# Rotary scores kernel: one GpSimd load and one GpSimd store around DMA engine 4 in place of five GpSimd loads

## The chip, the cores and the metric

The kernel runs on one core of a Trainium2 chip. The metric is the device time of one execution in microseconds (us): the median of three runs is 793.6 us (792.91 to 794.66). A difference between two kernels is told as a time and as a share of this.

## What is computed

From the reference, cut to what matters. `q` and `k` are [16, 512, 16, 64] in float32 (batch, sequence, heads, dim); `cos` and `sin` are [512, 32].

```
q1, q2 = q[..., :half_dim], q[..., half_dim:]
q_rot = np.concatenate([q1 * cos_q - q2 * sin_q, q1 * sin_q + q2 * cos_q], axis=-1)
...                                   (k_rot from k in the same way)
scores = np.einsum('bshd,bthd->bsht', q_rot, k_rot)
```

The inputs are 67 MB. The output, [16, 512, 16, 512] in float32, is 268 MB, so four fifths of all the bytes that move are stores of scores.

## The kernel before

**Tiling.** A batch of `q` or `k` is loaded by one transfer as 128 partitions of four sequence rows each, 16 KB to a partition, 2 MB in all (`load`, L113 to L122). Partition p holds the sequence rows 4p to 4p + 3; c counts these four. The work goes in 64 steps, i = 4 * batch + c. A step takes the 128 q rows of one c against all 512 k rows, for 16 heads, and fills one stage tile `st` of 128 partitions by 32 KB (4 MB), which one transfer stores to the output (`store`, L187 to L188).

**One step** (the last loop of the kernel): for each of eight pairs of heads `scores` (L190 to L213) has TensorE make two products of 64x128 by 64x512 into a PSUM tile `ps` (L201), and ScalarE copies both to `st` in one instruction of 128x1024 (L208). Between these, TensorE transposes later rows of q and k (L170), VectorE and ScalarE copy those from PSUM (L185), and VectorE makes the rotation in three operations on 128x1024 (L149, L150, L154). At the end of a step with c = 2 the next but one batch of q is loaded, and at the end of a step with c = 3 a batch of k; so step 18 issues the load of q6, step 19 that of k7, step 38 that of q11, step 39 that of k12 and step 54 that of q15 ("q6" is batch 6 of q).

**What sets the order.** The order of each engine's instructions is written out by hand (`manual_schedule`). Ordinary loads and stores are all issued by SyncE's queue in program order; each waits there for what it needs: a store for the last copy into its stage tile, a load for the last reader of its buffer. There are three stage tiles, so the first copy of step i waits until the store of step i - 3 has landed. q and k have two input buffers each. Steps 0 to 3 (batch 0) are stored in 16 pieces of 1 MB (L211) and loaded in smaller units; steps 4 to 63 make the 60 stores of L188.

**Engines and rows.** A transfer is carried by the core's DMA engines in parallel. A load or store of 128 rows gives each of the sixteen engines eight rows. The name `SLOW = 4` in the code (L75) is the number of one engine, and five loads are treated so that this one gets less:

- `RELIEVED` (L74) lists them: q6, k7, q11, k12, q15, numbered 0 to 4.
- `load_around` (L86 to L111) issues rows 0 to 119 of such a load on GpSimd's queue. A GpSimd transfer of 120 rows is carried by fifteen engines, eight rows each, that follow each other from a cursor; the cursor stands behind the last one afterwards. Before the first such load the cursor is reset (L101); `move_cursor(n)` (L78 to L84) shifts it by n engines with a tiny transfer of n rows into `scratch`, which nobody reads. `move_cursor(SLOW + 1)` sets it to 5, so the fifteen engines are 5 to 15 and 0 to 3.
- `halves` (L94 to L98) cuts each row of 16 KB in two pieces of 8 KB, the second first.
- The left rows 120 to 127: for a load with an even number (q6, q11, q15) SyncE issues them as a transfer of eight rows (L111); for an odd one (k7, k12) GpSimd issues them in halves, with the cursor set to 8 by `move_cursor(8)` (L105 to L107).

Of the kernel before, what the change touches and what calls it, by code (L numbers as in the profile page):

```python
# [10 lines left out]
def kernel(  # L11
# [8 lines left out]
    nc = tc.nc  # L20
# [4 lines left out]
    B, S, H, D = q.shape  # L25
    HD = D // 2
    P = 128
    C = S // P
# [14 lines left out]
    dram = {  # L43
        "q": q.rearrange("b (p c) h d -> b p c h d", c=C),
        "k": k.rearrange("b (p c) h d -> b p c h d", c=C),
    }
    o_v = out.rearrange("b (p c) h t -> b c p h t", c=C)
# [23 lines left out]
    batches = {}  # L71

    RELIEVED = {("q", 6): 0, ("k", 7): 1, ("q", 11): 2, ("k", 12): 3, ("q", 15): 4}  # L74
    SLOW = 4  # L75
    scratch = const_pool.tile([P, 96], fp32, name="scratch")
    tiny = [0]

    def move_cursor(n):

        y = tiny[0]
        tiny[0] += 1
        src = bass.AP(q.tensor, 512 * y, [(512, n), (64, 2), (1, 2)])
        nc.gpsimd.dma_start(scratch[:n, 4 * y : 4 * y + 4].rearrange("p (a b) -> p a b", a=2), src)  # L84

    def load_around(which, b, t):  # L86

        n, E, F = 120, C * H * D, C * H * D // 2  # L90
        x = RELIEVED[which, b]
        d = dram[which][b]

        def halves(lo, hi):  # L94
            src = bass.AP(d.tensor, d.offset + lo * E + F, [(E, hi - lo), (-F, 2), (1, F)])
            v = t[lo:hi].rearrange("p c e -> p (c e)")
            dst = bass.AP(v.tensor, v.offset + F, [v.ap[0], (-F, 2), (1, F)])
            nc.gpsimd.dma_start(dst, src)  # L98

        if x == 0:  # L100
            nc.gpsimd.inc_swdge_sem([], [], mode="reset_dge_cursor")  # L101
        else:

            move_cursor(16 - SLOW)
        if x % 2:  # L105
            move_cursor(8)
            halves(n, P)  # L107
        move_cursor(SLOW + 1)
        halves(0, n)
        if not x % 2:  # L110
            nc.sync.dma_start(t[n:].rearrange("p c (h d) -> p c h d", h=H), d[n:])  # L111

    def load(which, b):  # L113

        if b >= B:
            return
        t = in_pool.tile([P, C, H * D], fp32, tag=which + "_in", name=which + "_sb")
        batches[which, b] = t
        if (which, b) in RELIEVED:
            load_around(which, b, t)  # L120
        else:
            nc.sync.dma_start(t.rearrange("p c (h d) -> p c h d", h=H), dram[which][b])  # L122

# [61 lines left out]
        copy(out=dst, in_=src)  # L185

    def store(i, st):  # L187
        nc.sync.dma_start(o_v[i // C, i % C], st)  # L188

    def scores(i, p, st):  # L190

        ps = ps_s_pool.tile([P, 2, S], fp32, tag="ps_s", name="ps")
        b = i // C
        if b == 0:
            c, hp = divmod(p, 2)
            lhs, rhs = qT[i][:, C * hp + c], kT[0][:, 2 * i + hp]
        else:
            lhs, rhs = qT[i][:, p], kT[b][:, p]
        for r in range(2):
            po, rh = ps[:, r, :], rhs[64 * r : 64 * r + 64, :]  # L200
            nc.tensor.matmul(  # L201
                out=po, lhsT=lhs[64 * r : 64 * r + 64, :], rhs=rh, start=True, stop=True
            )
        so, si = st[:, 2 * p : 2 * p + 2, :], ps
        if b > 0:
            so = so.rearrange("s r (t c) -> s r t c", c=C)
            si = si.rearrange("s r (c t) -> s r t c", c=C)
        nc.scalar.copy(out=so, in_=si)  # L208
        if b == 0 and p % 2 == 1:
            c = p // 2  # L210
            nc.sync.dma_start(o_v[0, c, :, G * i : G * (i + 1)], st[:, G * c : G * (c + 1)])  # L211
        elif b > 0 and p == HP - 1:
            store(i, st)  # L213
# [9 lines left out]
    with tc.manual_schedule():  # L223
        for t, src in ((cos_t, cos), (sin_t, sin)):
            nc.scalar.dma_start(t, src.rearrange("(p c) j -> p c j", c=C))
        for head, heads in ((0, G), (G, H - G)):
            load_units("k", head, heads)
            load_units("q", head, heads)
        load("k", 1)
        load("q", 1)  # L230
        make_identity(nc, ident)
        nc.scalar.copy(out=ss_t[:, :, 0, :], in_=sin_t)
# [6 lines left out]
        for i in range(C):  # L239
            st = st_first[i] if i < 2 else stage_pool.tile([P, H, S], fp32, tag="stage", name="st")  # L240
            if i < C - 1:
                dve = rope("k", i + 1) + rope("q", i + 1) + rope("k", C + i)
                nxt = [("k", i + 1), ("q", i + 1)]
            else:
                dve = rope("q", C) + rope("k", C + i) + rope("q", C + 1) + rope("k", 2 * C)
                nxt = [("q", C), ("k", C + i)]
            for p in range(HP):
                scores(i, p, st)
                if p in (0, 1) and i > 0:
                    run(dve[:1])  # L250
                    dve = dve[1:]
                    transposed("k", C + i - 1, p, nc.vector.tensor_copy)
                if p == 3 and i < 2:
                    load("kq"[i], 2)
                if p in (2, 6):
                    m = len(dve) - (4 if p == 2 else 2) - (2 if i == C - 1 else 0)
                    run(dve[:m])
                    dve = dve[m:]
                    tr_act(*nxt.pop(0))
            run(dve)  # L260
# [3 lines left out]
        for i in range(C, NST):  # L264
# [10 lines left out]
            st = stage_pool.tile([P, H, S], fp32, tag="stage", name="st")  # L275
# [45 lines left out]
```

## Time and profile before

| | |
|---|---|
| runs, median (lowest to highest) | 793.6 us (792.91 to 794.66) |
| profiled execution, first to last instruction | 790.4 us, 3.2 us below the median of the runs |
| TensorE matmul busy | 684.4 us (87% of the span) |
| VectorE busy | 544.7 us (69%) |
| ScalarE busy | 562.0 us (71%) |
| GpSimd busy | 11.9 us (2%) |
| bytes moved by DMA | 336.18 MB, mean 425 GB/s |
| read from and written to HBM | 67.24 MB and 268.44 MB |
| stores of 4 MB: number, median time from issue to landing | 60, 24.7 us |
| loads on SyncE of 2 MB | 13 of k, 28.3 us; 12 of q, 26.5 us |
| loads on GpSimd of 1920 KB (120 rows) | 3 of q, 27.8 us; 2 of k, 43.3 us |

How to read it. The profile is that of one execution; its span runs from the first to the last instruction of the program, and the runs' time includes what lies around it. The busy share of an engine is a mean over all stages. The profile's page has the engines' busy shares in 40 slices of the span, and the mean busy share of the sixteen DMA engines in the same slices; a part on the DMA queues, where q1 is SyncE's queue and q0 GpSimd's; the chain of work that ended last; groups of equal instructions; and transfers with the time from issue to landing. The trace answers further questions: who waited for whom and how long, what was issued when, the busy times within a stretch of the span, and the records of the single DMA packets (start, duration, size and queue). A row of a transfer is one packet, or two when it is cut in halves.

### The profile page before, as it was taken

What the parts mean: (1) busy time and instruction counts of PE and PEld (TensorE: products, weight loads), DVE (VectorE), ACT (ScalarE), POOL (GpSimd) and SP (SyncE); (2) the same over time, 40 slices, a digit from 0 to 9 for tenths busy, and PEclk for the clock granted to TensorE, in tenths of its full rate; (3) what the DMA queues carried; (4) which work ended last, traced back from release to release, by engine and by line L of the source; (5) the groups of instructions that cost most, each with busy time, mean ns of one, the idle gap of its engine ahead of it and who ended that gap; (6) DMA issues with size and microseconds to landing.
All of it is one profiled execution on the core that took longest, in us unless ns stands there. A gap on an engine that the chain in (4) does not pass through costs nothing.

```text
span 790.4 us, 7750 instructions
## 1 busy us (share of the span) xinstructions
PE 684.4 (87%) x3072; PEld 296.4 (38%) x3072; DVE 544.7 (69%) x516; ACT 562.0 (71%) x647; POOL 11.9 (2%) x24
## 2 busy tenths in 40 slices
PE   4989998988988889798996989889899798799960
PEld 2444443433433334343342433334334343344420
DVE  6999988666766678576785767667678487587400
ACT  3888886865857768486785866777577586588770
POOL 0000000000001000000000001000000000000000
PEclk9999999998999999898998989999899899899995
DMA  9999999999999999999999999999999999999997
GB/s 357 417 425 439 429 430 435 425 435 436 429 429 428 413 432 419 433 423 438 433 427 436 426 432 429 422 432 424 430 432 427 436 429 432 430 432 434 432 429 340
DMA packets 18836, 336.18 MB, mean 425 GB/s; under 512 B 2312, under 2 KB 3592, under 8 KB 4616
## 3 DMA queue, kind: packets, MB, share of 16 engines
q1 hardware_dynamic: 16704, 325.46, 96.4%
q0 software_dynamic: 1808, 10.10, 3.1%
q8 instruction: 24, 0.39, 0.2%
q10 hardware_dynamic: 288, 0.13, 0.1%
q14 instruction: 12, 0.10, 0.0%
HBM read 67.24 MB, written 268.44 MB: 425 GB/s over the span
## 4 chain that ended last, share of the span: by engine, by line
DMA 49%; PE 40%; ACT 5%; DVE 3%; issue 1%; ACTq 0%; SPq 0%; DVEq 0%
DMA out_dram<-st 46%; PE ps L201 30%; PE bank L170 10%; ACT st L208 5%; DMA q_sb<-in_q_dram 2%; DVE part L149 1%; DMA early<-in_k_dram 1%; DVE q_sb L150 0%; DVE k_sb L154 0%; DVE k_sb L150 0%; DVE q_sb L154 0%; DVE early L150 0%; DVE kT_t L185 0%; ACTq L316 0%; DVE early L154 0%
## 5 line engine op out<-in xcount | busy, mean ns | idle before, releaser
L208 ACT COPY st<-ps 128x1024 f32<-128x1024 f32 x512 | 495.7, 1020 | 192.6 <-DMA out_dram<-st 109.8
L201 PE MATMUL ps<-kT_t,qT_t 64*128 64x512 f32 x2048 | 544.0, 649 | 67.0 <-ACT st L208 67.0
L201 PEld LDWEIGHTS ps<-kT_t,qT_t 64*128 64x128 f32 x2048 | 183.6, 196 | 256.2 <-issue 133.3
L185 DVE COPY qT_t<-bank 128x512 f32<-128x512 f32 x118 | 81.6, 691 | 193.9 <-PE bank L170 193.9
L170 PEld LDWEIGHTS bank<-ident,q_sb 128*128 128x128 f32 x480 | 54.2, 149 | 99.0 <-issue 96.4
L170 PEld LDWEIGHTS bank<-ident,k_sb 128*128 128x128 f32 x480 | 50.3, 140 | 96.4 <-DVE k_sb L150 39.5
L170 PE MATMUL bank<-ident,q_sb 128*128 128x128 f32 x480 | 85.1, 304 | 0.9 <-PE ps L201 0.9
L170 PE MATMUL bank<-ident,k_sb 128*128 128x128 f32 x480 | 78.5, 286 | 1.6 <-DVE qT_t L185 1.2
L185 ACT COPY kT_t<-bank 128x512 f32<-128x512 f32 x122 | 72.4, 598 | 6.4 <-PE bank L170 6.4
L154 DVE TENSOR_TENSOR k_sb<-k_sb,part 128x1024 f32<-128x1024 f32 x60 | 73.5, 1225 | 2.1
L150 DVE TENSOR_TENSOR q_sb<-q_sb,cos_t 128x1024 f32<-128x1024 f32 x60 | 73.5, 1225 | 2.1
L150 DVE TENSOR_TENSOR k_sb<-k_sb,cos_t 128x1024 f32<-128x1024 f32 x60 | 73.5, 1225 | 2.0
L149 DVE TENSOR_TENSOR part<-q_sb,ss_t 128x1024 f32<-128x1024 f32 x60 | 73.5, 1225 | 2.0
L149 DVE TENSOR_TENSOR part<-k_sb,ss_t 128x1024 f32<-128x1024 f32 x60 | 73.0, 1216 | 0.9 <-DMA k_sb<-in_k_dram 0.7
L154 DVE TENSOR_TENSOR q_sb<-q_sb,part 128x1024 f32<-128x1024 f32 x60 | 72.9, 1216 | 0.0
L170 PE MATMUL bank<-ident,early 128*128 128x128 f32 x64 | 10.5, 315 | 12.4 <-DVE early L154 10.5
L170 PEld LDWEIGHTS bank<-ident,early 128*128 128x128 f32 x64 | 8.3, 161 | 17.4 <-issue 13.4
L149 DVE TENSOR_TENSOR part<-early,ss_t 128x1024 f32<-128x1024 f32 x8 | 9.8, 1222 | 5.8 <-DMA early<-in_k_dram 5.7
L98 POOL DMA_DIRECT2D q_sb<-in_q_dram x3 | 2.3, 752 | 620.2 <-PE bank L170 446.2
L154 DVE TENSOR_TENSOR early<-early,part 128x512 f32<-128x512 f32 x16 | 10.3, 687 | 0.2
L150 DVE TENSOR_TENSOR early<-early,cos_t 128x1024 f32<-128x1024 f32 x8 | 9.8, 1225 | 0.3
L185 ACT COPY qT_t<-bank 128x512 f32<-128x512 f32 x10 | 5.7, 629 | 3.2 <-PE bank L170 3.2
(12 smaller groups left out, 15.9 us busy)
## 6 DMA issues: line engine op xcount, KB each, us to landing
out_dram<-st SPq DMA_DIRECT2D x60, 4096.0 KB, 24.7
k_sb<-in_k_dram SPq DMA_DIRECT2D x13, 2048.0 KB, 28.3
q_sb<-in_q_dram SPq DMA_DIRECT2D x12, 2048.0 KB, 26.5
out_dram<-st SPq DMA_DIRECT2D x16, 1024.0 KB, 13.8
q_sb<-in_q_dram POOLq DMA_DIRECT2D x3, 1920.0 KB, 27.8
k_sb<-in_k_dram POOLq DMA_DIRECT2D x2, 1920.0 KB, 43.3
early<-in_k_dram SPq DMA_DIRECT2D x1, 1536.0 KB
early<-in_q_dram SPq DMA_DIRECT2D x1, 1536.0 KB
```

Source lines behind the costliest of these rows:

```text
L98: nc.gpsimd.dma_start(dst, src)
L149: nc.vector.tensor_tensor(pv, xs, ss, op=mult)
L150: nc.vector.tensor_tensor(xc, xc, cs, op=mult)
L154: nc.vector.tensor_tensor(y, y, z, op=add)
L170: nc.tensor.transpose(bank[:, x, :], src, ident)
L185: copy(out=dst, in_=src)
L201: nc.tensor.matmul(out=po, lhsT=lhs[64 * r : 64 * r + 64, :], rhs=rh, start=True, stop=True)
L208: nc.scalar.copy(out=so, in_=si)
```

## The change

Only one load, q11, still goes around engine 4, as before: rows 0 to 119 in halves on GpSimd, the rows 120 to 127 by SyncE. q6, k7, k12 and q15 become ordinary loads of 128 rows on SyncE's queue. In their place the store of step 30 goes around it: rows 0 to 119 are issued on GpSimd in halves, 16 KB each here, with the cursor at 5, and the left rows by SyncE in two transfers of four rows, 120 to 123 and 124 to 127. The store comes first in program order, so the reset of the cursor stands before it, and q11 shifts the cursor by 12 and by 5. Of eighteen transfers on GpSimd's queue five are left: the two of 120 rows and three tiny ones. The function `load_around` becomes `around`, which takes a destination and a source.

```diff
-    RELIEVED = {("q", 6): 0, ("k", 7): 1, ("q", 11): 2, ("k", 12): 3, ("q", 15): 4}
     SLOW = 4
+    AROUND = 120
+    RELIEVED_LOADS = {("q", 11)}
+    RELIEVED_STORES = {30}
...
+    def around(dst, src):
+        def halves(t):
+            f = t.ap[1][1] // 2
+            return bass.AP(t.tensor, t.offset + f, [t.ap[0], (-f, 2), (1, f)])
+
+        if relieved[0] == 0:
             nc.gpsimd.inc_swdge_sem([], [], mode="reset_dge_cursor")
         else:
             move_cursor(16 - SLOW)
-        if x % 2:
-            move_cursor(8)
-            halves(n, P)
+        relieved[0] += 1
         move_cursor(SLOW + 1)
-        halves(0, n)
-        if not x % 2:
-            nc.sync.dma_start(t[n:].rearrange("p c (h d) -> p c h d", h=H), d[n:])
+        nc.gpsimd.dma_start(halves(dst[:AROUND]), halves(src[:AROUND]))
...
-        if (which, b) in RELIEVED:
-            load_around(which, b, t)
+        if (which, b) in RELIEVED_LOADS:
+            d = dram[which][b].rearrange("p c h d -> p (c h d)")
+            around(t.rearrange("p c e -> p (c e)"), d)
+            nc.sync.dma_start(t[AROUND:].rearrange("p c (h d) -> p c h d", h=H), dram[which][b][AROUND:])
...
     def store(i, st):
-        nc.sync.dma_start(o_v[i // C, i % C], st)
+        o = o_v[i // C, i % C]
+        if i in RELIEVED_STORES:
+            around(o.rearrange("p h t -> p (h t)"), st.rearrange("p h t -> p (h t)"))
+            for lo in (AROUND, AROUND + 4):
+                nc.sync.dma_start(o[lo : lo + 4], st[lo : lo + 4])
+        else:
+            nc.sync.dma_start(o, st)
```

More of the change, by code (lines that the diff above doesn't have):

```diff
@@ L71 @@
     batches = {}
-    RELIEVED = {("q", 6): 0, ("k", 7): 1, ("q", 11): 2, ("k", 12): 3, ("q", 15): 4}
     SLOW = 4
+    AROUND = 120
+    RELIEVED_LOADS = {("q", 11)}
+    RELIEVED_STORES = {30}
     scratch = const_pool.tile([P, 96], fp32, name="scratch")
     tiny = [0]
+    relieved = [0]
     def move_cursor(n):
@@ L84, in move_cursor @@
         nc.gpsimd.dma_start(scratch[:n, 4 * y : 4 * y + 4].rearrange("p (a b) -> p a b", a=2), src)
[L86 to L100, printed above, removed]
+    def around(dst, src):
[3 more added lines that the diff above has]
+        if relieved[0] == 0:
             nc.gpsimd.inc_swdge_sem([], [], mode="reset_dge_cursor")
```

## The prediction

> **What bounds the kernel now.** I read the page's second and third parts, then the waits, the stage windows, SyncE's timeline, and last the trace's packet records.
>
> ```profile
> span 790.4 us, 7750 instructions
> ...
> DMA  9999999999999999999999999999999999999997
> ...
> q1 hardware_dynamic: 16704, 325.46, 96.4%
> q0 software_dynamic: 1808, 10.10, 3.1%
> ```
>
> The first row is the span, DMA the busy share of the sixteen DMA engines in 40 slices. The queue rows (packets, MB, share of sixteen engines' span) add up with the three small ones to 99.8%: 788.8 of 790.4 us for the mean engine. No engine has time to spare, so the end is total work over sixteen, plus what the latest engine has more than the mean.
>
> ```profile
> ACT st L208 <- DMA out_dram<-st: 109.8, 42, 5.7
> SPq L188 <- ACT st L208: 659.7, 60, 16.7
> ...
> 225.00:310.00 85.00, 76.88 (x343) 32.74 (x340) 59.93 (x56) 62.45 (x73) 4.89 (x8) 0.94 1.00 424
> 310.00:381.00 71.00, 62.47 (x272) 26.71 (x272) 49.46 (x46) 49.32 (x57) 0.00 (x0) 0.90 1.01 432
> 767.00:790.00 23.00, 0.00 (x0) 0.00 (x0) 0.00 (x0) 0.83 (x1) 0.00 (x0) 0.53 0.84 360
> ```
>
> ScalarE waits 109.8 us for stage buffers that stores still read; SyncE has nearly always time. In the windows (the last three columns are clock, DMA share, GB/s) the stretch with the relieved loads q6 and k7 moves 424 GB/s against 432 after it: going around an engine is not free.
>
> The packet records have start, duration, size and queue, but no engine. On a busy engine the next packet starts 3 or 4 ns before the last one ends, so they can be strung into sixteen chains:
>
> ```
> 32 KB store packet  1213 ns; on one chain 1246 (median of the slow ones), from 30 to 767 us
> 16 KB load packet    611 ns;  8 KB GpSimd packet 309 ns
> slow chain against the median chain: +0.3 us at 75, +2.9 at 225, +0.5 at 318, +2.3 at 403,
>    +2.2 at 470, -1.6 at 561, 0.0 at 645, -1.8 at 707, -0.3 at 767
> last packets of the 16 chains: four at 783.6 to 784.3, the slow one near 787.2, the last 789.0
> ```
>
> The slow chain is the one without 8 KB packets when a relieved load runs: engine 4. It loses 33 ns on each store packet: 1.7 us in 100 us in the body ((2.9 - 0.3) / 150), 2.5 in 100 behind 707 (1.5 / 60), and the three groups of relieved loads give this back. At the end it stands in the middle. The last chains took no packet of q15's eight left rows, so they are of engines 8 to 15.
>
> **What each engine gains and loses.** I count in load rows of 16 KB, 0.611 us each, against an even split of 8 rows an engine.
> - Before: q6, q11, q15 give engine 4 one row of eight, k7 and k12 none: 3 x 7 + 2 x 8 = 37 rows less. Engines 0-3 and 5-7 have 3 more (the left rows of three q loads), 8-15 have 2 more (those of two k loads).
> - After: store 30 takes 8 rows of 32 KB from engine 4, that is 16; q11 takes 7: 23 less. Engines 0-3 get two 32 KB rows (the 4-row stores, taken as one row on each of the first four engines) and one of 16 KB: 5 more. Engines 5-7 have 1 more, 8-15 none.
> - Difference: engine 4 +14 rows = +8.6 us; engines 0-3 +1.2 us; 5-7 and 8-15 -1.2 us.
>
> **What goes with the four loads.** During a relieved load engine 4's store packets are stretched, by 200 to 400 ns each in the second half. Summed from the records: q6 2.1 us, k7 1.2, q11 2.0, k12 0.0, q15 1.7. Twice all engines stretch for about 3 us, at 258 and 504, where the 8-row GpSimd halves of k7 and k12 run: about 0.5 us an engine each time, 1.5 and 1.6 on engine 4. Gone from engine 4: 2.1 + 1.2 + 1.7 + 1.5 + 1.6 = 8.1 us. Gone from the others: 1.0 us. Eight small cursor transfers fewer (the 4 to 16 byte packets are 7 to 9 ns, two or three an engine) and 32 pairs of 8 KB packets an engine where one of 16 KB does (2 x 309 - 611 = 7 ns): 0.3 us an engine together.
>
> On the queues: k7 and k12 return to SyncE, where such loads waited 4.8 us in 6 cases, at most 0.8, inside SyncE's 659.7 us of waiting; below nothing it can't be, since GpSimd issued them at the same moment (246.8 and 248.0 against store 19 at 248.7). Two 4-row stores cost SyncE at most the 0.99 to 1.36 us of an 8-row load's issue each; behind them stands the load q9, and the queue is 9.6 us deep there (next paragraph). On GpSimd the store waits for ScalarE; behind it stand two small transfers and q11, not due for 90 us. Cost nothing.
>
> **The added store** is the unknown. It leaves SyncE's order:
>
> ```profile
> 364.82 16.76 SPq L188 DMA_DIRECT2D out_dram<-st  x2
> 381.69 0.67 SPq L122 DMA_DIRECT2D q_sb<-in_q_dram  x1
> 393.26 0.33 SPq L188 DMA_DIRECT2D out_dram<-st  x1
> ...
> 403.27 25.96 SPq L188 DMA_DIRECT2D out_dram<-st  x3
> ...
> 226.37 0.75 POOL L98 DMA_DIRECT2D q_sb<-in_q_dram  x1 [223.98 <-PE bank L170]
> ```
>
> Start, duration, engine, what is issued: the first row merges stores 29 (364.8) and 30 (381.25); the fourth is 32 to 34 (33 at 413.3). A GpSimd load issued at 226.37 had its first 8 KB packet at 230.94 (4.5 us), and its last landed at 255.24: each engine alternates one GpSimd packet with one of SyncE's, 16 x (309 + 1213) = 24.4 us. For the store the pieces are 16 KB: 16 x (609 + 1213) = 29.2 us. Engine 4 lags 2.9 + 1.56 x 1.7 = 5.6 us by then, so store 30 is issued about 1 us later, at 382.2, and lands at 382.2 + 4.5 + 29.2 = 415.9. In SyncE's order it landed at 403.5, when ScalarE began step 33. So step 33 starts 12 us later; with its 9.75 us (403.5 to 413.3) and about 1.5 us to the first packet, store 33 reaches the engines at 427.2. What is queued keeps the median engine busy to 430.2 (store 32's median landing) less the 1.1 us saved by then, 429.1. **The ring of three stage buffers covers the detour with 1.9 us to spare**; steps take 10 us where their transfers take 12, so the lost lead comes back.
>
> The loss X on engine 4 during the store: none if the stretch comes from writing SBUF (a store reads it); 9.8 us if all 16 row-times are lost; below nothing is excluded, since the relief is already counted whole. The nearest rows are the five transfers of 120 rows, 0 to 2.1 us, mean 1.4, which I take.
>
> **Sum**, from the ends of the chains:
> - engine 4: 787.2 + 8.6 - 8.1 - 0.3 + 1.4 = 788.8;
> - engines 8-15: 789.0 - 1.2 - 1.0 - 0.3 = 786.5;
> - engines 0-3, at most 787.7 now: + 1.2 - 1.0 - 0.3 = 787.6.
>
> The last goes from 789.0 to 788.8: -0.2 us. Span 790.2; the median of the runs, 793.6, lies 3.2 above the profiled span, and I take that over: 793.4, rounded down to **793.3** as the small stretches after 300 us may shrink too.
>
> [...] (32768 - 16384) bytes over 1213 - 611 ns is 27.2 bytes a ns, as if a fixed width bound each engine. [...]
>
> **Rivals.**
> 1. *The other engines rule* (X near 0, and a little more of the stretch gone than I counted): end 786.5 to 787.6, span 787.9 to 789.0, time 791.1 to 792.2. For it: k12 lost nothing, reads may not disturb. Against it: four of five transfers did.
> 2. *Engine 4 ends last*: loss by bytes, twice q11's: X = 4.0, engine 4 at 791.4, time 796.0. Engine 4 passes the old end of 789.0 from X = 1.6, and costs over 0.2% from X = 3.2.
> 3. *The stage ring runs dry*: if foreign and own reads of a store stretch each other, store 30 lands past 417.8 and each us beyond holds back all sixteen engines. 0.3 us on each of the 16 pairs (the stretch engine 4 showed) gives 4.8, less the spare 1.9: +2.9 us; with 0.6, +7.7. Time 796 to 801. Against it: nothing but engine 4 was stretched beside loads.
> 4. *It doesn't go around engine 4*: cursor or cut differ for a store. Then engine 4 lacks 9.8 us of relief: 788.8 + (9.8 - 1.4) = 797.2, time 801.8.
>
> **How the numbers follow.** Under 0.2% (1.6 us: 792.0 to 795.2), a measurement of this kernel can't be told from no change. Forecast 0.45 (of this 0.08 falls below 792.0, 0.05 above 795.2); rival 1 0.20; rival 2 0.15; rival 3 0.17; rival 4 0.03. Faster 0.08 + 0.20 = 0.28; same 0.32; slower 0.05 + 0.15 + 0.17 + 0.03 = 0.40. The forecast's own range is 792 to 795; rival 1 pulls the low end to 791.3, rivals 2 and 3 the high one to 797.5, with the worst of 3 and all of 4 left out.
>
> **What would show it.** In the changed profile: 240 GpSimd packets of 16 KB between 386 and 416 and none on the slow chain; store 30 landed near 416 and ScalarE's wait for stage buffers there some 12 us, with the DMA share still near 1.00 at 425 to 440 (rival 3: a dip, and 16 KB packets over 609 ns); no common stretch at 258 and 504; the slow chain within 2 us of the last one at the end (rival 2: alone and last). I am wrong if the unprofiled executions have another slow chain, or if engine 4's loss hangs on something the records don't show.

## The result and the profile after

The changed kernel takes **799.3 us** (798.94 to 799.64, five runs) where the kernel before takes 793.6 (792.91 to 794.66): a ratio of 1.0073, with a 95% interval of 1.0061 to 1.0085. It is slower by 5.7 us, and outside the range of 791.3 to 797.5. The profiled span went from 790.4 to 797.2 us.

First the page's rows that answer to those of before: span, DMA share in 40 slices of 19.9 us, GB/s in the same slices, and the two large queues.

```profile
span 797.2 us, 7728 instructions
...
DMA  9999999999999999999999999999999999999996
GB/s 355 425 424 437 435 427 436 421 439 429 428 435 429 434 428 428 437 425 433 364 362 409 424 437 432 423 429 434 431 435 427 433 433 428 437 428 437 428 433 299
...
q1 hardware_dynamic: 17120, 329.65, 97.1%
q0 software_dynamic: 640, 5.90, 2.1%
```

The DMA row is full to the end, as before. The row under it is not: three slices, from 379 to 438 us, move 364, 362 and 409 GB/s where the rest move some 430. That is where store 30 goes around engine 4. The same in the windows (the last three columns are clock, DMA share, GB/s):

```profile
310.00:381.00 71.00, 62.14 (x282) 26.92 (x282) 49.67 (x48) 50.44 (x59) 0.00 (x0) 0.95 1.00 430
381.00:430.00 49.00, 39.11 (x152) 16.13 (x152) 27.08 (x26) 27.74 (x32) 1.87 (x3) 0.83 1.00 367
430.00:470.00 40.00, 39.76 (x192) 17.30 (x190) 33.22 (x32) 34.28 (x41) 0.00 (x0) 1.00 1.00 430
```

The kernel before in the middle window:

```profile
381.00:430.00 49.00, 43.60 (x202) 18.75 (x198) 34.18 (x32) 35.18 (x41) 0.00 (x0) 0.97 1.00 431
```

After the change the DMA engines are busy all the time there (1.00), as before, but move 367 GB/s in place of 431. 49 us at 64 GB/s less is 3.1 MB, and at 430 GB/s that is 7.3 us. The DMA engines did not stand idle, so packets took longer. The packet records say which (start between 378 and 445 us; "stretch" is the time over 611 ns for a 16 KB and over 1213 ns for a 32 KB packet, added up over all sixteen engines):

```
                          before     after
GpSimd 16 KB packets        -        43.4 us (240 packets; median 611 ns, 95% below 1493, most 2292)
SyncE 32 KB store packets  2.2       57.3    (95% below 1918 ns, most 5233)
SyncE 16 KB load packets   0.6       10.7
sum                        2.8      111.4    = 7.0 us an engine, as the mean of sixteen
```

The medians are those of plain packets: a part of the packets is stretched, and strongly. Over the whole run the stretch (with it the time of 8 KB packets over 309 ns) went from 4.75 to 9.63 us an engine: 7.0 came here, and about 2 went with the four loads. That is 4.9 us more, and the mean end of the sixteen chains moved by 5.0, from 786.6 to 791.6. The last chain moved from 789.0 to 795.5; the 1.5 us between these are the last one's distance from the mean, which grew from 2.4 to 3.9. Three chains ended at 795.1 to 795.5. The slow one, engine 4, was not among them: it ended at 792.5.

The issues around the store in the changed kernel, SyncE's and then GpSimd's (start, duration, engine, line, what):

```profile
382.51 0.68 SPq L184 DMA_DIRECT2D out_dram<-st  x2
383.30 0.37 SPq L114 DMA_DIRECT2D q_sb<-in_q_dram  x1
398.50 0.35 SPq L186 DMA_DIRECT2D out_dram<-st  x1
...
415.81 24.70 SPq L186 DMA_DIRECT2D out_dram<-st  x3
...
382.80 0.75 POOL L101 DMA_DIRECT2D out_dram<-st  x1 [380.42 <-ACT st L206]
```

And ScalarE's first copies of steps 32 and 33 there (in brackets the idle time before them and what ended it):

```profile
404.21 2.84 ACT L206 COPY st<-ps 128x1024 f32<-128x1024 f32 x3 [5.74 <-DMA out_dram<-st]
...
419.51 3.94 ACT L206 COPY st<-ps 128x1024 f32<-128x1024 f32 x4 [3.72 <-DMA out_dram<-st]
```

Store 30 was issued on GpSimd at 382.8, had its first packet at 387.1 and landed at 419.4; ScalarE's first copy of step 33 follows at 419.5. Store 33, the second of the three in the merged row at 415.8, was issued at 430.2 (413.3 before). Step 33's wait for its stage buffer is 3.7 us long and cost nothing: the engines still had packets, as the share of 1.00 from 430 to 470 says.

### The profile page after: what moved, and what is told of

Its sections match the earlier page's. It is cut to its first block, busy times and chain, and to the rows that moved or that the text cites. A ratio compares the mean times of both kernels' runs of the same rounds, so it can differ in the third digit from the quotient of the medians.

```text
span 797.2 us, 7728 instructions
## 1 busy us (share of the span) xinstructions
PE 686.6 (86%) x3072; PEld 297.0 (37%) x3072; DVE 544.6 (68%) x516; ACT 561.6 (70%) x647; POOL 4.0 (1%) x11
## 4 chain that ended last, share of the span: by engine, by line
DMA 48%; PE 37%; DVE 5%; ACT 5%; issue 1%; ACTq 0%
DMA out_dram<-st 48%; PE ps L199 28%; PE bank L162 9%; ACT st L206 5%; DVE part L141 2%; DVE early L146 1%; DVE k_sb L142 1%; DVE k_sb L146 1%; DVE early L142 1%; DMA sin_t<-in_sin_dram 0%; DVE kT_t L177 0%; DVE q_sb L142 0%; DVE q_sb L146 0%; ACTq L314 0%; DVE qT_t L177 0%
## 5 line engine op out<-in xcount | busy, mean ns | idle before, releaser
L177 DVE COPY kT_t<-bank 128x512 f32<-128x512 f32 x6 | 4.1, 685 | 0.4 <-PE bank L162 0.4
```

## The experiments

Five theories are named in the expectations. **W**: two engines that read rows of a stage tile through one path at one time slow each other. **R**: the ring of three stage buffers runs dry, the mechanism of the third rival. **S**: the two 4-row stores do it. **G**: a store issued by GpSimd costs something of itself. **T**: a GpSimd store of fewer than 128 rows stretches whatever it reads. Each ratio is to runs of the kernel before that were made beside it.

### The loads without the store

```diff
-    RELIEVED_STORES = {30}          (in the changed kernel)
+    RELIEVED_STORES = set()
```

> Only q11 goes around engine 4; store 30 is an ordinary store, so the four removed loads are tested alone. All theories that put the loss into the store's detour (W: two engines read stage rows through one path; S: the two 4-row stores; G: a store issued on GpSimd as such; R: the ring of three stage buffers) expect no stretch between 381 and 430 us there: 428 to 432 GB/s, where the changed kernel moved 367. What is left is engine 4's lag: 787.2 + 8.6 + 9.8 - 8.1 - 0.3 = 797.2 by the ends of the chains of before, or by the drift 785.6 + 9.3 = 794.9, so a time of 799.5 to 802, engine 4 alone and last. If engine 4's drift were overcounted, 793 to 796.

Measured: 797.6 us (797.4 to 797.91), ratio 1.0049 [1.0034, 1.0064]; stretch 2.6 us.

```profile
381.00:430.00 49.00, 41.65 (x187) 17.65 (x184) 33.72 (x33) 33.53 (x40) 0.00 (x0) 0.93 1.00 429
...
767.00:790.00 23.00, 4.47 (x20) 1.20 (x16) 0.00 (x0) 6.04 (x7) 0.00 (x0) 0.68 0.82 355
```

The dip is gone (429 GB/s). The time is 2 us under the 799.5 to 802 expected. Engine 4 ends alone and last, as expected, at 794.2, while thirteen chains end between 785.8 and 786.5; the fall of the DMA share to 0.82 at the end is those that have finished. So dropping four relieved loads costs 3.8 us, and the detour of the store, which brings engine 4 back to the others, adds 1.7 to that instead of taking it away.

### Who issues it, and the left rows

Three edits to the changed kernel. The first issues all 128 rows of store 30 on GpSimd:

```diff
-            around(...)             (and the two 4-row stores)
+            nc.gpsimd.inc_swdge_sem([], [], mode="reset_dge_cursor")
+            nc.gpsimd.dma_start(halves(o...), halves(st...))
```

> Store 30 on GpSimd with all 128 rows in halves, so all sixteen engines carry their own share and engine 4 isn't spared; no 4-row stores. W expects no stretch if GpSimd deals the rows to the engines as SyncE does: over 425 GB/s between 381 and 430 us, and a time like that of the kernel without a relieved store. G expects the same loss as in the changed kernel, 367 GB/s, some 7 us over the kernel without a relieved store. R expects what the late landing costs (store 30 near 416 to 418), at most 1 us.

Measured: 800.95 us (798.59 to 802.77), ratio 1.0089 [1.0066, 1.0112]; stretch 2.6 us, the 256 GpSimd packets at 611 ns.

```profile
381.00:430.00 49.00, 44.42 (x200) 19.18 (x200) 34.12 (x32) 35.84 (x42) 1.44 (x2) 0.93 1.01 432
```

The same queue, the same halves and the same moment, and no stretch: being a GpSimd store is not what stretches packets. It is still 3.3 us above the kernel without it, which W did not expect, so G is not empty. Engine 4, relieved by q11 alone as there, is 10.4 us behind the median chain at the end (8.3 there); this profile, of the fastest of four runs, shows 1.2 us of the 3.3.

The second writes the left rows by one transfer of eight:

```diff
-            for lo in (AROUND, AROUND + 4):
-                nc.sync.dma_start(o[lo : lo + 4], st[lo : lo + 4])
+            nc.sync.dma_start(o[AROUND:], st[AROUND:])
```

> The changed kernel with the left rows 120 to 127 of store 30 as one transfer of eight rows on SyncE, one row on each of eight engines, engine 4 among them, in place of two transfers of four rows. S expects most of the stretch to go: 3 to 6 us faster than the changed kernel (793.5 to 796.5), and over 410 GB/s between 381 and 430 us. W expects the stretch to stay for the 240 packets: within 2 us of 799.3, under 390 GB/s.

Measured: 800.57 us (800.32 to 801.71), ratio 1.0089 [1.0074, 1.0104]; stretch 121.4 us, 362 GB/s. S falls: it expected 3 to 6 us less.

The third moves the places in HBM: the four steps of batch 7 write `out[7, P*(i%C) : P*(i%C+1)]`, that is, the output rows of that batch stand in another order.

> The changed kernel, but the four steps of batch 7 (28 to 31) write their 128 rows next to each other, 32 KB apart, in place of 128 KB apart; so the output rows of that batch stand in another order. W expects the same stretch between 381 and 430 us as in the changed kernel: 90 to 130 us of packet time over the plain durations, 360 to 375 GB/s. If the places in HBM that the shifted engines write make the stretch, it changes by over a third.

Measured, in a single run: 800.97 us; stretch 110.5 us, 368 GB/s. The stretch is that of the changed kernel, so the places in HBM are not its cause.

### The cut alone, on ordinary stores

These take the kernel before and cut store 30 into ordinary SyncE transfers, without GpSimd, cursor or relief:

```diff
-        nc.sync.dma_start(o_v[i // C, i % C], st)
+        o = o_v[i // C, i % C]
+        if i == 30:
+            for lo in (0, 64):                                        (rows cut at 64)
+                nc.sync.dma_start(o[lo : lo + 64], st[lo : lo + 64])
+        else:
+            nc.sync.dma_start(o, st)
```

> The kernel before with the ordinary store of step 30 cut in two transfers of 64 rows, both on SyncE, nothing else: no GpSimd, no engine spared, sixteen engines in each, four rows an engine. W (an engine that reads stage rows which are another engine's in a whole store shares a path with it): in each transfer sixteen engines read the rows of eight, so the 32 KB packets of this store stretch towards twice 1213 ns; an added 40 to 155 us of packet time over all engines between 395 and 420 us, 2.5 to 9.7 us on the time: 796 to 803. If the stretch is due to where in HBM the packets write, or to the GpSimd queue, nothing changes: within 1 us of 793.8.

Measured: 803.36 us (800.87 to 803.9), ratio 1.0116 [1.0099, 1.0133]; stretch 113.3 us.

```profile
381.00:430.00 49.00, 36.05 (x148) 14.97 (x144) 26.20 (x26) 26.35 (x30) 0.00 (x0) 0.83 0.99 366
```

The same dip as in the changed kernel, from a cut alone; the time is just above the 796 to 803 that W expected. The next cut is by columns, eight heads each and all 128 rows in both (`o[:, lo : lo + HP], st[:, lo : lo + HP]`):

> The kernel before with the ordinary store of step 30 cut by columns: two transfers of all 128 rows with eight heads (16 KB a row) each, on SyncE. Each engine reads the rows that it has in the whole store. W expects no stretch: within 1 us of 793.5 and under 5 us of added packet time between 378 and 445 us, where the cut by rows (the same bytes, the same two transfers of 2 MB) added 113 us and took 9.9 us more. If a cut store costs as such, the 10 us come again (800 to 804).

Measured: 793.58 us (792.2 to 795.2), ratio 1.0001 [0.9991, 1.0011]; stretch 2.7 us.

```profile
381.00:430.00 49.00, 43.35 (x200) 18.57 (x196) 34.20 (x32) 35.54 (x41) 0.00 (x0) 0.97 1.01 432
```

Two transfers are harmless; two that split the rows are not. Then the rows in even and odd ones (`o[lo::2], st[lo::2]`):

> The kernel before with store 30 cut in two transfers of 64 rows on SyncE, the even rows and the odd rows. If an ordinary store deals blocks of eight rows in a row to an engine, each engine reads only rows of its own block here, and nothing stretches (under 5 us, 793.5). If it deals smaller groups, of four rows say, engines share groups as in the cut at row 64 (113 us added), 40 to 120 us added and 797 to 804.

Measured, in a single run: 794.1 us; stretch 2.7 us, 431 GB/s. So it is not the number of rows either, but which rows a transfer takes. By its expectation this spoke for blocks of eight; two runs below overturn that. The same with a load, q9 as rows 0 to 63 and 64 to 127:

> The kernel before with the ordinary load q9 cut in two transfers of 64 rows on SyncE. If writes to SBUF share such a path as reads do, the 16 KB packets stretch towards twice 611 ns: 20 to 78 us of added packet time over all engines near 400 us and 1.3 to 4.9 us on the time (795 to 798.5). If only reads do, within 1 us of 793.8 and under 5 us of added packet time.

Measured: 796.64 us (795.37 to 797.36), ratio 1.0035 [1.0022, 1.0049]; stretch 37.3 us, of it 33.6 on the 16 KB load packets; 412 GB/s. A load, which writes SBUF, stretches by such a cut as well.

Two more cuts put the blocks of eight to the test. Eight transfers of sixteen rows (`o[lo::8], st[lo::8]`):

> The kernel before with store 30 cut into eight ordinary SyncE transfers of sixteen rows, j, 8+j, ... 120+j, all sixteen engines, one row each. [...] Blocks: an ordinary store gives engine e the rows 8e to 8e+7; then every piece is the engine's own and nothing stretches: under 15 us between 378 and 445, about 430 GB/s, 793 to 795 us. [...]

Measured: 801.25 us (800.4 to 802.13), ratio 1.0099 [1.0084, 1.0114]; stretch 100.4 us.

```profile
381.00:430.00 49.00, 38.55 (x168) 15.87 (x166) 27.56 (x27) 30.57 (x35) 0.00 (x0) 0.91 1.00 374
```

And four of 32 rows (`o[lo::4], st[lo::4]`):

> The control: the kernel before with store 30 cut into four SyncE transfers of 32 rows, j, 4+j, ... 124+j. [...]

Measured: 794.35 us (792.14 to 795.08), ratio 1.0008 [0.9998, 1.0018]; stretch 2.9 us.

```profile
381.00:430.00 49.00, 43.09 (x186) 18.18 (x182) 32.90 (x32) 33.43 (x39) 0.00 (x0) 0.90 1.01 432
```

Had an engine its eight consecutive rows, the cut by eight would have been the harmless one. It stretches (100.4 us), and the cuts by two and by four don't (2.7 and 2.9). From here on the author took it that what an engine owns goes by groups of four rows, and that fewer rows are dealt in the pattern of 128: a reading that agrees with these runs and is not shown by them, as the packet records name neither rows nor engines.

### The detour with other owners

The changed kernel with the cursor at 0 for the store (no move ahead of it; `move_cursor(SLOW + 2)` ahead of q11), to give engines 0 to 14 the rows of blocks 0 to 14:

> The changed kernel with the cursor at 0 for the store, so engines 0 to 14 carry rows 0 to 119, eight in a row each, engine 4 too, and engine 15 is spared; the two 4-row stores stay. If an ordinary store deals rows in blocks of eight (rows 0 to 7 on engine 0), each engine now reads its own rows: W expects the 240 GpSimd packets at 609 ns and a stretch only on the rows of the 4-row stores, 4 to 7 us faster in the stretch, with engine 4's missing relief (9.8 us) given back at the end: 798 to 803. If an ordinary store deals rows in another pattern, W expects the stretch to stay (under 390 GB/s) and a time of 803 to 810. S expects the stretch to stay whatever the cursor.

Measured: 806.12 us (804.41 to 807.03), ratio 1.0149 [1.013, 1.0168]; stretch 116.3 us; engine 4 is last, 8.1 behind the median chain. A miss for W with blocks of eight, as it was held then; the expectation's other case, another pattern, is met. Which rows of a whole store an engine carries was not shown.

Before the cut by eight was run, the same was tried row by row. For each j of 0 to 7, eleven rows from 40+j in steps of eight go to engines 5 to 15 and four rows from j to engines 0 to 3:

```diff
-            around(...)
+            for j in range(8):
+                move_cursor(SLOW + 1 if j == 0 else 1)
+                nc.gpsimd.dma_start(halves(dst[40 + j :: 8]), halves(src[40 + j :: 8]))
+                nc.gpsimd.dma_start(halves(dst[j:32:8]), halves(src[j:32:8]))
+            nc.sync.dma_start(o[32:40], st[32:40])
```

> The changed kernel with one edit: store 30 still goes around engine 4 on GpSimd's queue in halves, but in eight pairs of transfers that are meant to leave each engine its own block of eight consecutive rows: rows 40+j, 48+j, ... 120+j (eleven rows) with the cursor at 5, then j, 8+j, 16+j, 24+j (four rows) on engines 0 to 3, a move of the cursor by 1 behind each pair; SyncE stores the left rows 32 to 39. Theory W (time is lost where two engines read the same rows' share of the stage tile at one time): stretch of the packets between 378 and 445 us below 20 us against 111.5 in the changed kernel, 425 to 432 GB/s between 381 and 430; time 792 to 797 us (799.3 less 7.0 is 792.3, and the 3.4 to 3.7 us of a GpSimd store as such, seen twice, may stay). Theory T, that a GpSimd store of fewer than 128 rows stretches whatever rows its engines take, as the run with the cursor at 0 suggests: 90 to 120 us of stretch, 365 GB/s, 798 to 801 us.

Measured: 820.63 us (818.76 to 822.22), ratio 1.0344 [1.0329, 1.0358]; stretch 100.1 us. Its control, fifteen rows `j:120:8` for each j instead of the eleven and four:

> The control to the kernel before it in this call: eight transfers of fifteen rows j, 8+j, ... 112+j with the cursor at 5, a move by 1 behind each, so that engines 5 to 15 and 0 to 3 take the blocks 0 to 14, each engine another one's block; SyncE stores rows 120 to 127. Cut and number of pieces are like there, only the owners differ. W and T both: 90 to 120 us of stretch, about 365 GB/s, 798 to 802 us. If this one has no stretch either, the cut into small transfers has taken it away, and W is not shown by the pair.

Measured: 817.74 us (815.41 to 820.67), ratio 1.0311 [1.029, 1.0333]; stretch 106.3 us. And the first of these beside the five relieved loads of before:

> The kernel before with its five relieved loads, and store 30 going around engine 4 as in the first kernel of this call (each engine its own rows). W: stretch below 20 us, 425 to 432 GB/s; time 792 to 794 if the GpSimd store costs nothing of itself, 796 to 797 with the 3.7 us that the store of 128 rows on GpSimd cost beside the five loads. T: as the five loads with the detour of the change, 800 to 802.

Measured: 819.08 us (817.62 to 823.71), ratio 1.0341 [1.0317, 1.0365]; stretch 98.4 us. The stretch of the first and the third is a miss for W with blocks of eight. All three times are misses, for a reason of their own. GpSimd's queue in the first, from its eighth transfer on (in brackets the idle time before and what ended it):

```profile
386.93 0.60 POOL L192 DMA_DIRECT2D out_dram<-st  x1
393.48 0.54 POOL L86 DMA_DIRECT2D scratch<-in_q_dram  x1 [5.96 <-DMA out_dram<-st]
397.07 0.58 POOL L191 DMA_DIRECT2D out_dram<-st  x1 [3.05 <-DMA out_dram<-st]
```

And its windows:

```profile
381.00:430.00 49.00, 30.68 (x128) 12.85 (x126) 21.95 (x22) 22.83 (x27) 11.45 (x20) 0.81 1.00 384
430.00:470.00 40.00, 33.05 (x144) 13.75 (x142) 24.20 (x24) 25.43 (x30) 2.86 (x5) 0.89 0.76 292
```

Eight transfers go out at once, from 382.95 to 386.93; from the ninth on each waits until an older one has landed. The last GpSimd packet of the store ended at 454.6, and then the stage ring did run dry: the DMA share falls to 0.76. This is what theory R looks like, and what the changed kernel does not show.

By the reading of groups of four the detour was dealt once more, still in halves from the cursor at 5, with rows four apart in each transfer: for each j of 0 to 3 rows 52+j, 56+j, ... to 92+j, then 32+j to 44+j, and so on; SyncE stores the left rows 16 to 19 and 48 to 51 in two transfers:

> [...] 28 transfers stand in GpSimd's queue, which held back the run with 23 of them (it let eight be under way at a time), so the time will again be 810 to 840 us and tells nothing; the packets tell. [...] Blocks, or a GpSimd store that stretches whatever it reads: 80 to 120 us, as the 112 us of the two runs before it.

Measured: 820.74 us (819.87 to 823.59), ratio 1.0351 [1.0331, 1.0371]; stretch 106.4 us, which as a sum speaks for blocks or for T. But the packet records fall into two parts. The first 106 GpSimd packets, which start from 387.5 to 416.0 us, take 611 to 629 ns each:

```
stretch of the first 106 GpSimd packets of store 30, all engines
changed kernel                22.8 us
dealt by blocks of eight      11.3
the control to it              7.4
dealt by groups of four        0.04
```

So a GpSimd store of fewer than 128 rows does not stretch whatever it reads: T falls as it is worded. What stretches in this part is mostly on SyncE: eight store packets that start between 387.4 and 399.2 take 4.1 to 10.2 us, 46.1 us over eight plain ones. Eight is the number of the left rows that SyncE stores; the records don't name rows, so that these are the eight is argued and not shown. From 416 us on GpSimd's packets stretch too, up to 2.6 us, and why stays open.

### The relieved loads beside it

Back to the five loads. The kernel before with the detour of store 30 added:

```diff
+        if i == 30:
+            move_cursor(16 - SLOW)
+            move_cursor(SLOW + 1)
+            nc.gpsimd.dma_start(halves(dst[:120]), halves(src[:120]))
+            for lo in (120, 124):
+                nc.sync.dma_start(o[lo : lo + 4], st[lo : lo + 4])
```

> The kernel before with its five relieved loads, and store 30 around engine 4 as in the changed kernel: the detour of the store alone, with engine 4 relieved twice. W expects the same 100 to 120 us of added packet time between 378 and 445 us, 6.3 to 7.5 us an engine, and as no other engine gains by the further relief, 799.5 to 801.5. If the changed kernel lost its time by engine 4's lag and not by the stretch, 792 to 795.

Measured: 801.81 us (800.72 to 809.19), ratio 1.0138 [1.0088, 1.0188]; stretch 111.4 us. The time is just above the 799.5 to 801.5 that W expected. The detour, with the loads left as they were, costs 8.6 us by the medians; one run of 809.2 among four makes the interval wide (7.0 to 14.9 us). All 128 rows on GpSimd in its place (`nc.gpsimd.dma_start(halves(dst), halves(src))`):

> The kernel before with its five relieved loads, and store 30 issued on GpSimd in halves, but with all 128 rows, so that each engine carries its own share: the control for the detour (801.8 us with fifteen engines). W expects under 5 us of added packet time between 378 and 445 us and a time within 1 us of the kernel before. G (a store issued on GpSimd costs by itself, by its order or its late landing) expects the 3.4 us again by which the sixteen-engine store lay over the kernel with q11 alone: 796 to 798.

Measured: 796.54 us (795.44 to 798.11), ratio 1.0041 [1.0028, 1.0055]; stretch 19.8 us, 421 GB/s. So of the 8.6 us some 3.7 come with the GpSimd store as such, as G expected, and about 5 with the way its rows are dealt. W expected under 5 us of stretch here, and 19.8, or 1.2 an engine, is a miss. In the profiled run, the slowest of five, one chain ends last, 7.6 us above the median one. Why is open.

Last the kernel before with the left rows of k7 and k12 by SyncE, that is without their 8-row GpSimd halves, where all engines stretched at 258 and 504:

> The kernel before, with the left eight rows of k7 and k12 issued by SyncE as those of the three q loads, in place of GpSimd halves on engines 8 to 15. The common stretch at 258 and 504 us goes if those halves make it: 0.5 us an engine each time; engines 8 to 15 carry two rows less (1.2 us), engines 0 to 3 and 5 to 7 two more. By the ends of the chains the last goes from 789.0 to 787.9: 1.1 us faster, 792.7 beside 793.8. If the stretch has another cause, 793.5 to 794.5.

Measured: 793.21 us (792.48 to 794.42), ratio 0.9997 [0.9988, 1.0006]. In the 3 us there the stretch fell from 8.5 to 1.1 and from 7.1 to 1.6 us, and the time stayed: another chain was the last one, 3.8 us above the median. So the common stretch does come from those halves, and of the 1.1 us expected 0.3 came, not clear of zero.

## Why the prediction was wrong

**What bounds it** was right: DMA, with a DMA share near 1.00 before and after.

**Rows and engine 4's drift** were near enough for the store's moment and not for the end. Engine 4 was 6.6 us behind at 380 (5.6 predicted). Carried over to the kernel without the detour, the sum gives 787.2 + 30 x 0.611 - 8.1 - 0.3 = 797.1, and it ended at 794.2: about 3 too high. With this store's mean loss of 7.0 us for X in place of 1.4 the sum for the changed kernel would be 788.8 - 1.4 + 7.0 = 794.4, and engine 4 ended at 792.5, about 2 too high. What engine 4 gets back or loses outside the counted rows is not known that well. That eight rows on SyncE's queue go to engines 0 to 7, and four to 0 to 3, was the author's assumption. The 3.2 us from the profiled span to the median was 2.1 after the change: each listed run lies about 1.75 us above its own span, and the rest is the distance of the profiled run from the median.

**The common stretch** of the 8-row halves at 258 and 504 is gone in the changed kernel, as predicted; that alone moves no end.

**Queues and issue times** show no cost, as predicted: SyncE issued the two 4-row stores in 0.68 us. The first packet came 4.3 us after the issue (4.5 taken).

**"The added store" is the step that failed.** It was put at 16 x (609 + 1213) = 29.2 us, landing at 415.9, with a loss X of 1.4 us on engine 4 alone. It landed at 419.4, and the loss was 7.0 us an engine in the mean of all sixteen, 111.4 us in sum, of which 43.4 lie on the very packets that go around engine 4. The step took rows of the profile that belong to another case: GpSimd's 8 KB packets ran at 309 ns beside SyncE's stores, but those packets write SBUF while stores read it. What the added store does, reading a stage tile's rows dealt otherwise than in a whole store, beside whole stores, no row of before showed. Cuts of an ordinary store have a stretch of the same size, 113.3 us where rows are cut at 64 and 100.4 by eights, or none to speak of, 2.7 to 2.9 by columns, twos and fours. The bound of 0 to 9.8 us for X was also put on engine 4 alone; the fifteen engines that carry the store got no term for it, and it is three of them that end last.

**The third rival** had an origin that the cuts agree with, foreign and own reads stretching each other, and the wrong carrier. It let the lost time pass through the stage ring, free up to a landing at 417.8. But the stretched packets were lost DMA time from the first on (7.0 us an engine at a share of 1.00); the ring did not run dry (share 1.00 from 430 to 470), and no spare covers it. That its 796 to 801 us holds the measured time is luck: it was worked out from the landing and the spare, and the time was lost another way.

**The forecast by ends of chains** had engine 4 last or level. In the changed kernel it is 0.9 us above the mean; the last three are others, up to 3.9 above the mean.

**What stays open**: whether two engines share a path, as W has it, which no record names; why the detour dealt by groups of four stretches from 416 us on, and so whether a whole detour without stretch exists; how much of the changed kernel's stretch is due to its left rows; the 3.3 to 3.7 us of a 128-row GpSimd store; why engine 4's store packets take 33 ns more. No kernel here beats the one before by more than its measurement can tell.

## What to carry to other kernels

Where DMA is the bound, count packet durations and GB/s, not the busy share: a share of 1.00 was the same at 430 and at 367 GB/s. Sending rows around an engine, and cutting a transfer by blocks of rows, stretched packets here, its own and others (111.4 us in the changed kernel, 113.3 for a store and 37.3 for a load cut at row 64); try a cut by columns, which cost nothing here (2.7 us), sooner than blocks of rows. And a price read from packets that write SBUF (8 KB at 309 ns) did not hold for packets that read it (43.4 us over plain on 240).

## What the runs showed of the hardware

- A 4 MB store cut at row 64 into two transfers costs 9.9 us (1.0116 [1.0099, 1.0133]); by columns nothing (1.0001 [0.9991, 1.0011]); by steps of four rows nothing that can be told (1.0008 [0.9998, 1.0018]); by steps of eight 7.9 us (1.0099 [1.0084, 1.0114]).
- The 2 MB load cut at row 64 costs 3.2 us, with 37.3 us of stretch, a third of the store's.
- Fewer than 128 rows on GpSimd can run unstretched: the first 106 packets of the store dealt by groups of four take 611 to 629 ns, where the first 106 of the changed kernel take up to 2273.
- Not every packet is stretched by a fixed share: in the changed kernel the median stays at 611 and 1213 ns, and single packets take up to 2292 and 5233 ns.
- Rows sent around an engine: in the kernel before, the 240 packets of 8 KB of q15's rows 0 to 119 (670.9 to 692.3 us) lie sixteen each on fifteen chains; the slow chain has none, and carries 4-byte packets of GpSimd's queue there. With the cursor at 5 for store 30 engine 4 ended 0.9 us above the mean chain, with it at 0 it ended 8.1 behind the median one.
